# Row factors and diagonal blocks of a triangular matrix, taken chunk by chunk with the products that make it, in a hybrid decoder block on one Trainium2 core

## The chip, the cores and the metric

The kernel runs on one core of one Trainium2 chip. Its metric is device time in microseconds (us) of one execution. All times below are us unless they say ns.

## The reference, cut to what matters

One decoder layer over 512 tokens of width 1024: a combined input projection feeds three causal mixers (A: block-sparse attention, B: a chunked gated delta rule, C: sparse attention with an indexer that picks top keys), gates weigh their outputs, then come an output projection, a layer norm, and a squared-ReLU MLP with a second layer norm. The part at issue is mixer B, 4 heads of 128 columns. Per chunk it needs the inverse of a unit lower triangular matrix:

```python
q = to_chunks(q) * dk ** -0.5            # q, k are l2-normalised rows
diff = g[..., :, None] - g[..., None, :]
decay = jnp.where(causal, jnp.exp(jnp.where(causal, diff, 0.0)), 0.0)
kb = k * beta[..., None]
m = jnp.where(strict, -jnp.einsum('bhncd,bhnsd->bhncs', kb, k) * decay, 0.0)
tinv = lax.linalg.triangular_solve(eye - m, jnp.broadcast_to(eye, m.shape),
                                   left_side=True, lower=True, unit_diagonal=True)
u = jnp.einsum('bhncs,bhnse->bhnce', tinv, v * beta[..., None])
w = jnp.einsum('bhncs,bhnsd->bhncd', tinv, kb * jnp.exp(g)[..., None])
```

The kernel works with chunks of 128 tokens and unnormalised keys and queries, and puts the norms in as factors: a row factor beta / (k.k + eps) on the triangular matrix, and a factor on the query's result that is (q.q + eps) to the power -1/2, times 128 to the power -1/2.

## The kernel before, in words

**Matmuls and the stream.** Each large matmul is three fp32r matmuls (`mm3`, L91 to L93) on the high and low halves of both operands. `split` (L75) makes the halves of a weight: ACT casts (L76, tile `wh`), then DVE or POOL subtracts (L80, tile `wl`); `share` says how often POOL gets that. The projections are a stream of pieces: a piece loads one 128x1024 weight, runs 24 matmuls of 512 columns into a bank of `pj` (three buffers, as `wh` and `wl` have), and an eviction follows, for the gates an ACT operation on L173 (L176 for two of them). `weave(steps, n)` (L144) emits a list of steps with n pieces spread between them.

**Order.** Program order is only a priority. When the program is built, each engine's instructions are put into a fixed order by a scheduler that expects some duration of each: an instruction whose inputs are not yet expected lets later ones pass. On the chip each engine then works through its order, and waits at its head. So the top-k of the indexer (L413 and L414 on DVE), which comes later in the program, stands between the steps described here, and so do the halves of weights.

**The triangular stage**, for four chunks c of four heads each, 16 units u = 4c + h:

- `decays(c)` (L470) makes on DVE the masks R (L476), on PE the sums of log decays, on ACT their exponentials EA (L482, masked on POOL, L483) and EG (L488).
- `products(c)` (L492) has PE multiply keys with keys into the only `ov` bank (L499) and keys with queries into a `tr` bank (L501). DVE reads the diagonals of the first into `kk` (L503, one operation per head), multiplies by EA into LT (L505), and likewise into AT (L511). PE turns the queries (L508), ACT squares and sums them into `qq` (L510). DVE scales the queries by EG (L512). The steps are woven with GDEC = 2 pieces (L519).
- Behind the last chunk, DVE adds eps to `kk` and `qq` (L521, L522), takes the reciprocal and multiplies by beta (L523, L524: `br2`) and multiplies the four chunks of LT by it (L527). POOL raises `kk` to 1/2 (L529: `nk`) and `qq` to -1/2 (L530: `rq`); DVE scales `rq` by 128 to the -1/2 (L531); POOL multiplies the values by `nk` (L534).
- The 32x32 diagonal blocks of LT are copied into LD, doubled, by ACT and DVE, 32 partitions of 1024 elements each, two copies an engine (L543). DVE transposes LD into FB (L546) and runs 31 steps of forward substitution, two operations a step (L558, L560), into XB. Two transposes (L568, L570) give XY; ACT and DVE copy from it into XL (L572) and Y (L574).
- Only then does the program emit `weave([], GPRE)` (L576) with GPRE = 8 pieces. The levels of the block inverse follow, `q32` to `z64` (L584 to L617, the first product is L589), with two pieces between them, and the recurrence over the chunks (L626 to L686) with two more.

`rq` is used in the recurrence (L674), `nk` through the values (L648), `br2` in L652.

Of the kernel before, what the change touches and what calls it, by code (L numbers as in the profile page):

```python
# [10 lines left out]
F32 = mybir.dt.float32  # L11
F32R = mybir.dt.float32r
AF = mybir.ActivationFunctionType
OP = mybir.AluOpType
# [8 lines left out]
RMS_EPS = 1e-6  # L23
# [31 lines left out]
def hybrid_block(ctx, tc, xT, xn, wt, wva, wsm, wuk, wuv, wbr, wout, wup, wdn, relb, onehot, cmats,  # L55
                 convw, alog, dtb, gnorm, kvnorm, ikg, ikb, l1g, l1b, l2g, l2b, out):
    nc = tc.nc
    PE, DVE, ACT, POOL = nc.tensor, nc.vector, nc.scalar, nc.gpsimd
# [131 lines left out]
    gp = gctx.enter_context(tc.tile_pool(name="gp", bufs=1))  # L190
# [65 lines left out]
    v3 = lambda a: a.rearrange("p (h c) -> p h c", h=4)  # L256
# [81 lines left out]
    p = bank("pj")  # L338
# [6 lines left out]
    p = bank("tr")  # L345
# [7 lines left out]
    beta = const.tile([128, 16], F32, name="beta")  # L353
# [36 lines left out]
    for i in range(NT):  # L390
        DVE.tensor_scalar(kin[:, i, :64], sm[:, i, :64], kag[:, i, 0:1], krs[:, i:i + 1],
                          op0=OP.subtract, op1=OP.mult)
# [4 lines left out]
    p = bank("tr")  # L397
# [32 lines left out]
    for j in range(4):  # L430
        weave([lambda h=h, i=i: index_score(h, i) for h in (2 * j, 2 * j + 1) for i in range(1, NT)], 1)
        if j == 0:
            p = bank("tr")
# [23 lines left out]

    LT = gp.tile([128, 16, 128], F32, name="LT", tag="b8", bufs=4)
    AT = gp.tile([128, 16, 128], F32, name="AT", tag="b8", bufs=4)
    el = const.tile([128, 16], F32, name="el")  # L460

    scl = const.tile([128, 6, 16], F32, name="scl")
    kk, qq, nk, rq, br2 = (scl[:, i] for i in range(5))
    junk = gp.tile([128, 128], F32, name="junk")
    junk2 = gp.tile([128, 128], F32, name="junk2")
    hs = [slice(128 * h, 128 * h + 128) for h in range(4)]
# [25 lines left out]
    def products(c):  # L492
        cs = slice(128 * c, 128 * (c + 1))
        us = slice(4 * c, 4 * c + 4)
        EA, EG = dec[c]
        pQ = bank("tr")
        pK = bank("ov")
        for h in range(4):
            PE.matmul(pK[:, 128 * h:128 * h + 128], kT[:, h, cs], kT[:, h, cs], start=True, stop=True)  # L499
        for h in range(4):  # L500
            PE.matmul(pQ[:, 128 * h:128 * h + 128], kT[:, h, cs], qT[:, h, cs], start=True, stop=True)  # L501
        for h in range(4):
            DVE.scalar_tensor_tensor(junk, pK[:, hs[h]], 1.0, ident, op0=OP.mult, op1=OP.mult,  # L503
                                     accum_out=kk[:, 4 * c + h:4 * c + h + 1])
        DVE.tensor_tensor(LT[:, us], v3(pK), EA, OP.mult)  # L505
        p = bank("sc")
        for h in range(4):
            PE.transpose(p[:, hs[h]], qT[:, h, cs], ident)  # L508
        for h in range(4):
            ACT.activation(junk2, p[:, hs[h]], AF.Square, accum_out=qq[:, 4 * c + h:4 * c + h + 1])  # L510
        DVE.tensor_tensor(AT[:, us], v3(pQ), EA, OP.mult)  # L511
        DVE.tensor_tensor(qT[:, :, cs], qT[:, :, cs], EG, OP.mult)  # L512
# [5 lines left out]
    steps.insert(TV3, lambda: turn_value(3))  # L518
    weave(steps, GDEC)  # L519

    DVE.tensor_scalar(kk, kk, RMS_EPS, None, op0=OP.add)  # L521
    DVE.tensor_scalar(qq, qq, RMS_EPS, None, op0=OP.add)  # L522
    DVE.reciprocal(br2, kk)  # L523
    DVE.tensor_tensor(br2, br2, beta, OP.mult)  # L524
    for c in range(4):
        us = slice(4 * c, 4 * c + 4)
        DVE.tensor_tensor(LT[:, us], LT[:, us], bh(br2[:, us]), OP.mult)  # L527
    phalf, mhalf16 = pows[:, 0], pows[:, 1]
    POOL.tensor_tensor(nk, kk, phalf, OP.pow)  # L529
    POOL.tensor_tensor(rq, qq, mhalf16, OP.pow)  # L530
    DVE.tensor_scalar(rq, rq, 128.0 ** -0.5, None, op0=OP.mult)  # L531
    for c in range(4):
        us = slice(4 * c, 4 * c + 4)
        POOL.tensor_tensor(v3(vn[:, c]), v3(vn[:, c]), bh(nk[:, us]), OP.mult)  # L534
# [1 line left out]

    blk = [slice(32 * k, 32 * k + 32) for k in range(4)]
    LD = gp.tile([128, 32, 32], F32, name="LD", tag="LD")  # L540
    FB = gp.tile([128, 32, 32], F32, name="FB")
    for k, bs in enumerate(blk):
        (DVE.tensor_copy if k % 2 else ACT.copy)(  # L543
            LD[bs].rearrange("p c (h u) -> p c h u", h=2),
            LT[bs, :, bs].rearrange("p u c -> p c u")[:, :, None, :].to_broadcast([32, 32, 2, 16]))
    DVE.transpose(FB.rearrange("p c s -> p (c s)"), LD.rearrange("p c l -> p (c l)"))  # L546
    XB = gp.tile([128, 16, 32], F32, name="XB")
    TB = gp.tile([128, 512], F32, name="TB")
# [658 lines left out]
```

## Time and profile before

| what | value |
|---|---|
| median of 3 runs | 1024.02 us (1023.84 to 1025.14) |
| the profiled execution, its own time | 1024.51 us |
| its span, first to last instruction | 1022.7 us |
| mean granted PE clock | 0.968 |
| PE busy | 982.6 us, 96% of the span |
| DVE, ACT, POOL busy | 582.5, 416.6, 295.7 us |
| the chain that ended last, by engine | PE 74%, DVE 18%, ACT 3%, issue 2%, POOL 1%, DMA 1% |

The span is that of the profiled execution, and 1.8 us of its own time lie around it. A row of a timeline gives start, duration, engine, line, operation, output and inputs with their shapes, and in brackets how long the engine idled before it and what ended that. A row of the chain gives start, duration and what ran. Tile names are those of the program without buffer numbers; the views kk, qq, nk, rq and br2 show as their tile `scl`, the queries as `y_q_b` and the keys as `y_k_b`. Matmul ends are modelled and overlap the next start.

### The profile page before, as it was taken

To read this page: it belongs to the slowest core of one execution; us is meant where nothing else is said; L and a number is where in the kernel's file an instruction comes from. 1 tells how busy PE (TensorE), PEld (TensorE's weight loads), DVE (VectorE), ACT (ScalarE), POOL (GpSimd) and SP (SyncE) were. 2 spreads that over 40 slices of the span, in tenths; PEclk is the share of its full clock that TensorE was granted. 3 is DMA by queue.
4 is the path that set the end of the run, shared out by engine and by line. 5 is a ranking of instruction groups with operands and counts; after the bars stand their busy time and mean duration, and the time that the engine had idled before them with its cause. 6 is when DMAs were issued, how large, how long until landed. Compare 5 with 4: busy or idle time off the path is not lost.

```text
span 1022.7 us, 12939 instructions
## 1 busy us (share of the span) xinstructions
PE 982.6 (96%) x4868; PEld 807.7 (79%) x4868; DVE 582.5 (57%) x1145; ACT 416.6 (41%) x745; POOL 295.7 (29%) x194
## 2 busy tenths in 40 slices
PE   7999988979999999999999999999999999999997
PEld 4778876756788878878788888898888888888886
DVE  4969999793144657898975666842320222222236
ACT  4545435413124655776665353234332123333120
POOL 0202513521023223134443333224331013442111
PEclk9999998977599999999999999999999999999999
DMA  6385221133112321222334567223223323323312
GB/s 201 119 113 155 86 79 53 62 124 94 41 53 81 95 78 52 78 72 94 104 116 146 181 192 253 76 101 110 99 87 103 101 86 102 103 83 103 99 66 83
DMA packets 37931, 105.46 MB, mean 103 GB/s; under 512 B 5068, under 2 KB 9837, under 8 KB 37869
## 3 DMA queue, kind: packets, MB, share of 16 engines
q1 hardware_dynamic: 35804, 101.49, 30.1%
q10 hardware_dynamic: 2064, 3.15, 2.4%
q8 instruction: 38, 0.62, 0.2%
q14 instruction: 25, 0.20, 0.1%
HBM read 93.09 MB, written 11.53 MB: 102 GB/s over the span
## 4 chain that ended last, share of the span: by engine, by line
PE 74%; DVE 18%; ACT 3%; issue 2%; POOL 1%; DMA 1%; SPq 0%; DVEq 0%; ACTq 0%; POOLq 0%
PE pj L91 18%; PE pj L93 18%; PE pj L92 18%; DVE wl L80 2%; DVE isc L414 2%; DVE m L413 2%; PE sc L91 2%; PE sc L93 2%; PE sc L92 2%; PE tr L91 1%; PE tr L93 1%; PE tr L92 1%; PE tr L753 1%; PE sc L317 1%; PE sc L318 1%
## 5 line engine op out<-in xcount | busy, mean ns | idle before, releaser
L80 POOL TENSOR_TENSOR wl<-wraw,wh 128x1024 fp32r<-128x1024 f32 (+2 forms) x57 | 132.8, 2330 | 353.2 <-ACT wh L76 344.2
L76 ACT CAST wh<-wraw 128x1024 fp32r<-128x1024 f32 (+3 forms) x144 | 147.5, 1024 | 212.7 <-PE pj L92 101.5
L91 PE MATMUL pj<-xh,wh 128*128 128x512 f32 (+1 forms) x472 | 200.7, 426 | 3.4 <-ACT gate L173 2.0
L93 PE MATMUL pj<-xh,wl 128*128 128x512 f32 (+1 forms) x472 | 192.5, 408 | 8.0 <-DVE wl L80 6.3
L80 DVE TENSOR_TENSOR wl<-wraw,wh 128x1024 fp32r<-128x1024 f32 (+2 forms) x87 | 114.0, 1311 | 138.2 <-ACT wh L76 136.6
L92 PE MATMUL pj<-xl,wh 128*128 128x512 f32 (+1 forms) x472 | 190.8, 404 | 1.4 <-DVE xl L80 1.4
L93 PEld LDWEIGHTS pj<-xh,wl 128*128 128x128 f32 (+1 forms) x472 | 92.1, 195 | 31.1 <-DVE wl L80 8.1
L91 PEld LDWEIGHTS pj<-xh,wh 128*128 128x128 f32 (+1 forms) x472 | 91.7, 195 | 20.6 <-ACT gate L173 2.5
L92 PEld LDWEIGHTS pj<-xl,wh 128*128 128x128 f32 (+1 forms) x472 | 92.3, 196 | 16.3 <-DVE xl L80 3.3
L91 PE MATMUL pj<-x1h,wh 128*128 128x512 f32 (+1 forms) x280 | 104.0, 371 | 0.0
L92 PE MATMUL pj<-x1l,wh 128*128 128x512 f32 (+1 forms) x280 | 103.8, 371 | 0.0
L93 PE MATMUL pj<-x1h,wl 128*128 128x512 f32 (+1 forms) x280 | 103.8, 371 | 0.0
L1056 DVE TENSOR_TENSOR hl<-hraw,hh 128x512 fp32r<-128x512 f32 x32 | 22.2, 693 | 92.4 <-ACT hh L1055 92.4
L1053 POOL TENSOR_TENSOR hraw<-hraw 128x512 f32<-128x512 f32 x32 | 45.4, 1419 | 81.0 <-ACT hraw L1052 81.0
L93 PEld LDWEIGHTS pj<-x1h,wl 128*128 128x128 f32 x280 | 52.7, 188 | 9.1
L92 PEld LDWEIGHTS pj<-x1l,wh 128*128 128x128 f32 x280 | 52.8, 188 | 9.0
L91 PEld LDWEIGHTS pj<-x1h,wh 128*128 128x128 f32 x280 | 52.7, 188 | 9.0
L741 ACT ACTIVATE P<-P,ast 128x128 f32<-128x128 f32 (+1 forms) x64 | 36.0, 563 | 31.7 <-DVE ast L740 31.0
L1055 ACT CAST hh<-hraw 128x512 fp32r<-128x512 f32 x32 | 19.9, 621 | 67.6 <-POOL hraw L1053 67.6
L743 DVE TENSOR_SCALAR P<-P,ast 128x128 f32<-128x128 f32 (+1 forms) x64 | 34.5, 541 | 1.5
L736 POOL TENSOR_TENSOR bm<-strip,isc 128x256 f32<-128x256 f32 (+2 forms) x24 | 24.3, 1021 | 37.3 <-DVE ast L740 28.3
L759 DVE TENSOR_TENSOR ptl<-tr,pth 128x128 fp32r<-128x128 f32 (+1 forms) x64 | 30.5, 485 | 4.1 <-ACT pth L758 3.7
(376 smaller groups left out, 1990.5 us busy)
## 6 DMA issues: line engine op xcount, KB each, us to landing
wraw<-in_wt_dram SPq DMA_DIRECT2D x58, 512.0 KB, 3.3
wraw<-in_wup_dram SPq DMA_DIRECT2D x32, 512.0 KB, 3.3
wraw<-in_wdn_dram SPq DMA_DIRECT2D x32, 512.0 KB, 3.2
gdram<-gate SPq DMA_DIRECT2D x24, 256.0 KB, 2.0
wraw<-in_wbr_dram SPq DMA_DIRECT2D x12, 512.0 KB, 3.4
g<-gdram SPq DMA_DIRECT2D x24, 256.0 KB, 3.1
wraw<-in_wout_dram SPq DMA_DIRECT2D x8, 512.0 KB, 3.7
rrep<-rrow ACTq DMA_DIRECT2D x1, 3072.0 KB, 33.8
```

The lines of the kernel that those rows point to most:

```text
L76: ACT.copy(h, raw)
L80: eng.tensor_tensor(l, raw, h.bitcast(F32), OP.subtract)
L91: PE.matmul(out_ap, lh, rh, start=first, stop=False)
L92: PE.matmul(out_ap, lh, rl, start=False, stop=False)
L93: PE.matmul(out_ap, ll, rh, start=False, stop=last)
L413: DVE.max(m8, sc)
L736: POOL.tensor_tensor(bm[:, :n], bias, self.masks[i], OP.add)
L741: ACT.activation(P, P, AF.Exp, bias=mi[:, 0:1], scale=-1.0, accum_out=mi[:, 2:3])
L743: DVE.tensor_scalar(P, P, mi[:, 3:4], None, op0=OP.mult)
L759: DVE.tensor_tensor(dest(self.ptl), pv, dest(self.pth).bitcast(F32), OP.subtract)
L1053: POOL.tensor_tensor(a, a, a, OP.mult)
L1056: DVE.tensor_tensor(tl, a, th.bitcast(F32), OP.subtract)
```

## The change

The row factors br2 are made inside `products(c)` for the chunk's four columns, and the product of the keys is multiplied by its row factor and by EA in one operation per head. The chunk's part of the diagonal blocks is copied into LD there, by ACT (blocks 0 and 2) and by POOL (blocks 1 and 3; before: DVE), 32 partitions of 256 elements each. The four products behind the last chunk go, as do the common eps, reciprocal and beta operations. The factor 128 is multiplied into `qq` together with eps, ahead of the power -1/2, and L531 goes.

```diff
     LT = gp.tile([128, 16, 128], F32, name="LT", tag="b8", bufs=4)
     AT = gp.tile([128, 16, 128], F32, name="AT", tag="b8", bufs=4)
+    blk = [slice(32 * k, 32 * k + 32) for k in range(4)]
+    LD = gp.tile([128, 32, 32], F32, name="LD", tag="LD")
...
-        DVE.tensor_tensor(LT[:, us], v3(pK), EA, OP.mult)
+
+        DVE.tensor_scalar(kk[:, us], kk[:, us], RMS_EPS, None, op0=OP.add)
+        DVE.reciprocal(br2[:, us], kk[:, us])
+        DVE.tensor_tensor(br2[:, us], br2[:, us], beta[:, us], OP.mult)
+        for h in range(4):
+            u = 4 * c + h
+            DVE.scalar_tensor_tensor(LT[:, u], pK[:, hs[h]], br2[:, u:u + 1], EA[:, h], op0=OP.mult, op1=OP.mult)
+        for k, bs in enumerate(blk):
+            (POOL.tensor_copy if k % 2 else ACT.copy)(
+                LD[bs].rearrange("p c (h u) -> p c h u", h=2)[:, :, :, us],
+                LT[bs, us, bs].rearrange("p u c -> p c u")[:, :, None, :].to_broadcast([32, 32, 2, 4]))
...
-    DVE.tensor_scalar(kk, kk, RMS_EPS, None, op0=OP.add)
-    DVE.tensor_scalar(qq, qq, RMS_EPS, None, op0=OP.add)
-    DVE.reciprocal(br2, kk)
-    DVE.tensor_tensor(br2, br2, beta, OP.mult)
-    for c in range(4):
-        us = slice(4 * c, 4 * c + 4)
-        DVE.tensor_tensor(LT[:, us], LT[:, us], bh(br2[:, us]), OP.mult)
+    DVE.tensor_scalar(qq, qq, RMS_EPS, 128.0, op0=OP.add, op1=OP.mult)
     phalf, mhalf16 = pows[:, 0], pows[:, 1]
     POOL.tensor_tensor(nk, kk, phalf, OP.pow)
     POOL.tensor_tensor(rq, qq, mhalf16, OP.pow)
-    DVE.tensor_scalar(rq, rq, 128.0 ** -0.5, None, op0=OP.mult)
...
-    blk = [slice(32 * k, 32 * k + 32) for k in range(4)]
-    LD = gp.tile([128, 32, 32], F32, name="LD", tag="LD")
     FB = gp.tile([128, 32, 32], F32, name="FB")
-    for k, bs in enumerate(blk):
-        (DVE.tensor_copy if k % 2 else ACT.copy)(
-            LD[bs].rearrange("p c (h u) -> p c h u", h=2),
-            LT[bs, :, bs].rearrange("p u c -> p c u")[:, :, None, :].to_broadcast([32, 32, 2, 16]))
```

## Rows read from the trace of the kernel before

**Rows 1.** Timeline of PE, 177 to 238 us
```profile
177.81 1.16 PE L499 MATMUL ov<-y_k_b 128*128 128x128 f32 x8 [1.19 <-DVE LT L505]
...
198.20 0.50 PE L93 MATMUL pj<-xh,wl 128*128 128x512 f32 x1 [0.42 <-POOL wl L80]
...
205.04 0.50 PE L91 MATMUL pj<-xh,wh 128*128 128x512 f32 x1 [1.56 <-ACT gate L173]
...
206.99 0.79 PE L93 MATMUL pj<-xh,wl 128*128 128x512 f32 x1 [1.21 <-POOL wl L80]
...
208.86 0.63 PE L91 MATMUL pj<-xh,wh 128*128 128x512 f32 x1
...
218.74 0.80 PE L93 MATMUL pj<-xh,wl 128*128 128x512 f32 x1 [4.59 <-DVE wl L80]
...
236.84 0.39 PE L93 MATMUL pj<-xh,wl 128*128 128x512 f32 x1
237.16 0.43 PE L589 MATMUL sc<-XL,LT 32*32 32x32 f32 x8
```

**Rows 2.** Chain of waits, pieces between 184 and 218 us
```profile
184.12 3.89 POOL scl L529
...
193.59 5.70 DVE LT L527 x4
...
217.47 1.23 DVE wl L80
```

**Rows 3.** Timeline of ACT, 199 to 238 us
```profile
199.33 4.10 ACT L543 COPY LD<-LT 32x1024 f32<-32x1024 f32 x2 [10.11 <-DVE LT L527]
203.45 1.04 ACT L76 CAST wh<-wraw 128x1024 fp32r<-128x1024 f32 x1
...
213.56 1.05 ACT L76 CAST wh<-wraw 128x1024 fp32r<-128x1024 f32 x1 [5.70 <-PE pj L92]
...
232.95 2.21 ACT L572 COPY XL<-XY 32x512 f32<-32x512 f32 x2 [17.85 <-DVE XY L568]
...
236.46 1.05 ACT L76 CAST wh<-wraw 128x1024 fp32r<-128x1024 f32 x1
```

**Rows 4.** Timeline of DVE, 183 to 210 us
```profile
183.27 0.69 DVE L505 TENSOR_TENSOR LT<-ov,EA 128x512 f32<-128x512 f32 x1
183.87 0.17 DVE L521 TENSOR_SCALAR scl<-scl 128x16 f32<-128x16 f32 x1
...
190.92 1.01 DVE L531 TENSOR_SCALAR scl<-scl 128x16 f32<-128x16 f32 x1 [5.51 <-POOL scl L530]
...
203.57 1.23 DVE L546 STREAM_TRANSPOSE FB<-LD 128x1024 f32<-128x1024 f32 x1
...
207.46 2.39 DVE L558 TENSOR_TENSOR TB<-FB,XB 128x30 f32<-128x30 f32 x1
209.88 0.19 DVE L560 TENSOR_TENSOR XB<-XB,TB 128x30 f32<-128x30 f32 x1
```

**Rows 5.** Timeline of POOL, 190 to 210 us
```profile
190.86 4.49 POOL L534 TENSOR_TENSOR vn<-vn,scl 128x512 f32<-128x512 f32 x4
195.31 2.84 POOL L80 TENSOR_TENSOR wl<-wraw,wh 128x1024 fp32r<-128x1024 f32 x1
...
207.43 2.37 POOL L80 TENSOR_TENSOR wl<-wraw,wh 128x1024 fp32r<-128x1024 f32 x1 [0.50 <-ACT wh L76]
```

**Rows 6.** Groups: L503 and L727 (ns min/median/max), top-k from 184 us
```profile
L503 DVE SCALAR_TENSOR_TENSOR junk<-ov,cm x16: 267/280/1829, 156.4 to 183.1; 128x128 f32<-128x128 f32 x16
...
L413 DVE MAX8 m<-isc 128x8 f32<-128x512 f32 x3 | 2.1, 685 | 0.0
L414 DVE MATCH_REPLACE8 isc<-m,isc 128x512 f32<-128x512 f32 x3 | 2.0, 677 | 0.0
...
L727 POOL COPY strip<-far x16: 390/404/866, 317.6 to 521.6; 128x256 f32<-128x256 f32 x16
```

**Rows 7.** PE, PEld, DVE, ACT, POOL busy, PE clock, DMA share, GB/s, 245 to 281 us
```profile
245.00:281.00 36.00, 36.00 (x205) 25.02 (x204) 5.88 (x14) 5.81 (x12) 2.37 (x1) 0.50 0.14 49
```

## The prediction

> **What bounds the kernel now.** I read the page first: TensorE (PE) is the busiest engine by far, so the end moves only where PE idles or runs at its lower clock. I then read PE's timeline around the triangular stage for its idle gaps, the chain of waits for what stood behind them, and the timelines of ACT, DVE and POOL for what those had queued.
>
> PE works through eight stream pieces (24 matmuls each) between the products of chunk 3 and the first level product at 237.16, which starts right behind the last matmul of the eighth piece [rows 1]. So PE does not wait for the triangular chain there. It loses time earlier: 1.56 at 205.04 behind a gate eviction on ACT, 1.21 at 206.99 behind a `wl` on POOL, 4.59 at 218.74 behind a `wl` on DVE. After the second and third gaps the matmuls of 512 columns take 0.63 (the one at 208.86) against 0.39 at full clock (236.84) [rows 1]; 7 and 11 of them do. As each overlaps the next, I count 0.2 for one. A piece at full clock is 5.5: from 218.74 to 236.84 lie 69 matmuls, 11 of them slow, so (18.1 - 2.2) / 69 = 0.23 each, times 24.
>
> The chain of waits says why. From 184 to 217 it does not run through PE: two powers on POOL from 184.12 (3.89 the first), the four LT products (5.70), the substitution, and then the DVE `wl` that ends PE's longest gap [rows 2]. On ACT, the two LD copies wait 10.11 for LT and take 4.10, and the weight cast at 203.45 stands behind them; that makes the first two gaps [rows 3]. On DVE, L531 holds the queue for 5.51 until the second power is there, although only the query factor needs it, and the row factors of LT come after it [rows 4].
>
> **The change, part by part.**
>
> *Query factor inside the power.* L531 goes, 1.01 long, and with it the 5.51 that DVE waits [rows 4]; the 128 joins an existing operation, at no cost. The powers stay on POOL. What is late next is not DVE but the POOL queue.
>
> *Row factors with the products.* The four LT products (5.70) go [rows 2]. In their place each chunk has three operations on four columns (0.17 each by L521 [rows 4], 0.5 in sum) and four 128x128 products with a column scalar, priced by L503, the same form and shape, with a median of 280 ns [rows 6]: 1.1 in place of L505's 0.69 [rows 4]. That is 0.9 more per chunk, 2.7 before the keys' product of chunk 3, which already waits 1.19 for LT of chunk 2 to give its bank back [rows 1].
>
> *LD copies by chunk.* ACT's two copies, 4.10 for both at 32x1024 [rows 3], become eight of a quarter, 0.5 each; only chunk 3's pair, 1.0, remains behind the last LT. DVE's two go to POOL as eight. No row shows a POOL copy of 32 partitions with this stride; the nearest is the 128x256 copy, 0.39 to 0.87, median 0.40 [rows 6]. Bounds: 0 (hidden) and 0.87 each; I take 0.4, the median of the same element count. A POOL copy can also hold DVE up: the substitution product at 207.46 took 2.39 (the next, 0.19) while POOL's `wl` at 207.43 took 2.37 [rows 4, 5]. So the four copies of chunks 0 and 1 add 0 to 1.6 to DVE before chunk 3's keys.
>
> On this the Trainium skill ("SBUF — State Buffer", Who interferes with whom) speaks against the change: a DVE instruction with two SBUF inputs, or a copy in a two-port mode, and a GpSimd instruction that reads SBUF exclude each other for a whole instruction. The trace agrees, with 2.39 beside 2.37 [rows 4, 5]. By it all eight copies would stop DVE, about 3.2 us instead of my 1.6, if each fell on such an instruction, and the sum below would be up to 1.6 higher.
>
> *Where the chain then stands.* LT of chunk 3 ended at 183.96 [rows 4]; four times 0.9 and some contention put it at 188 to 190. With ACT's pair FB could start at 191. But the first power is ready before LT of chunk 3, so POOL probably takes it, perhaps both, ahead of its two copies: 6.7 for both (184.12 to the values at 190.86 [rows 2, 5]) from about 187, and 0.8 of copies, give 195; with the four value products (4.49 [rows 5]) in front as well, 199. FB started at 203.57 [rows 4]: 4.5 to 12 earlier, and I take 8. XL, copied from 232.95 to 235.16 [rows 3], is then there by 223 to 231, for a PE that wants it near 230: covered.
>
> *What PE gets.* (a) The gaps at 205.04 and 206.99 came from ACT standing in LD; they go, with 7 slow matmuls: 1.56 + 1.21 + 1.4 = 4.2 less. Bounds 0 and 4.2; the wait that made them is removed, so 4.2. (b) The `wl` at 217.47 sits in DVE's order among the substitution steps. If it keeps its place it comes 8 earlier and PE's 4.59 + 2.2 go; but a chain expected earlier puts more steps ahead of it. Bounds 0 and 6.8; I leave 1.5 standing and take 5.3 less. (c) The wait for chunk 3's keys grows by 0 (other matmuls put in front) to 4.3 (2.7 + 1.6); I take 1.5, nearer the low end, since PE has stream pieces to go on with. (d) POOL's `wl` at 195.31 stands behind the powers and the value products [rows 5], and PE already waits 0.42 for it [rows 1]; POOL begins them 2.7 later and has 0.8 of copies more, PE is 1.5 later itself: 0 to 3.5 less PE's own shift, I take 1.0.
>
> The sum: 4.2 + 5.3 - 1.5 - 1.0 = 7.0 less. From 237 on PE is nearly always busy, so this reaches the end. The profiled execution took 1024.51, 0.5 above the median of 1024.02: 1017.5.
>
> **The rivals.**
>
> *One cast stuck behind XL: no change.* ACT's XL copy now waits 17.85 for the substitution, and the cast at 236.46 stands behind it; the cast at 213.56 was the last ahead of it [rows 3]. Each engine's order is fixed when the program is built. If the chain is expected earlier by more than the distance between that cast and the XL copy, the cast of the eighth piece falls behind XL. Then XY at 225, XL 2.2, cast 1.05, `wl` 2.37 give weights near 230.6; PE wants them at 230 less one piece of 5.5, so it idles about 6 and has 2.2 of slow matmuls: 8 of loss against 7 of gain, 1025; with FB 12 earlier, 1021. Middle 1023. For it: it is the mechanism that LD shows now. Against: the order may move less than one cast.
>
> *Two casts behind XL: slower.* The same place, but the order shifts by over one piece (5.5), so that the seventh piece's weights wait too: PE idles about 11.4 and has 2.2 of slow matmuls, 13.6 against 7 of gain: 1031, or 1027 with FB 12 earlier. It decides from the point where two casts follow XL on ACT. Against it: LT, L531 and LD together must look over 5.5 us shorter to whoever orders the queues, and the products' stage gets longer.
>
> *DVE late in the products' stage.* The three small operations and the products depend on one another, and top-k operations of 0.68 can be let in between: six of them stand after 184 now [rows 6], so 4.1 can move ahead. With 2.7 and 1.6 that is 8.4 before chunk 3's keys; with 2.2 of slow matmuls and 1.0 from (d) it makes 11.6, against 11.0 from (a) and (b) in full: 1025.1. Against it: PE has stream pieces to put in front.
>
> *The clock of the level products.* From 245 to 281 the granted clock is 0.50, the level of 1.2 GHz, with PE busy for all 36.00 [rows 7], so some 18 could come back. Nothing in the change alters that mix; a shift of the order could move its beginning by some us.
>
> **How the numbers follow.** Forecast 0.48; one cast stuck 0.20; two casts 0.17; DVE late 0.10; the clock 0.05 (by 3 to 18 faster). About 0.2% is what a measurement of this kernel can tell from no change, 2 us. Faster: 0.48 + 0.05 + a third of the stuck cast, 0.60. Same: the rest of that rival and half of DVE late, 0.20. Slower: two casts and what is left, 0.20. The forecast's own range is 1012 (the waits of 1.19 and 0.42 gone too, 12.6 less) to 1021; the whole range, 1011 to 1027, takes in one stuck cast, late DVE and the lower edge of two.
>
> **What would show each step.** DVE without a wait for the powers and FB before 196: the chain is right; FB at 199 or later: POOL's queue holds its copies. The gate eviction no longer behind LD, and no gap near 205: (a). A `wl` gap under 2 in the substitution: (b). A keys' product waiting over 4 for LT: DVE late. ACT's cast straight after XL with PE idle before it: a stuck cast. The forecast is wrong if PE's gaps between 180 and the first level product still add up to 7 or more.

## The result, and the profile after

Four executions of the changed kernel took 1006.16, 1006.94, 1024.09 and 1024.38 (median 1015.51), beside 1023.34 to 1025.14 for the kernel before (median 1023.93). The comparison gives 0.9834 of the time before, interval 0.9809 to 0.9858; it rests on the two near 1006.5, and a number in the middle, such as the median, is one that no execution took. The mean granted clock of PE parts the two pairs: 0.987 and 0.966. The kernel before showed one group only: 69 executions beside the runs below, 1021.46 to 1027.78, clock 0.963 to 0.971.

The profiled execution of the changed kernel is one of the upper pair: own time 1024.38, span 1022.4, clock 0.967, PE busy 982.6 again. So it shows what the change did to the chain, and where that was lost. Its line numbers are shifted by the edit: LT is on L513, the LD copies on L515, the powers on L535 and L536, the values on L539, FB on L545, the substitution on L557, XL on L571, Y on L573, the first level product on L588 and the first product of the recurrence on L629.

PE's timeline, 146 to 277, to be set against [rows 1] (L501 is the product of keys with keys, chunks 0, 2 and 3 in turn):

```profile
146.62 1.05 PE L501 MATMUL ov<-y_k_b 128*128 128x128 f32 x8
...
175.12 1.16 PE L501 MATMUL ov<-y_k_b 128*128 128x128 f32 x8 [1.97 <-DVE LT L513]
...
177.08 0.78 PE L487 MATMUL sc<-R,cr 128*128 128x512 f32 x1 [0.57 <-ACT EA L484]
...
186.51 1.05 PE L501 MATMUL ov<-y_k_b 128*128 128x128 f32 x8
...
214.43 0.61 PE L93 MATMUL pj<-xh,wl 128*128 128x512 f32 x1 [4.18 <-DVE wl L80]
...
232.12 0.43 PE L588 MATMUL sc<-XL,LT 32*32 32x32 f32 x8
234.47 0.50 PE L91 MATMUL pj<-xh,wh 128*128 128x512 f32 x1 [1.92 <-ACT gate L173]
234.81 0.40 PE L92 MATMUL pj<-xl,wh 128*128 128x512 f32 x1
235.24 0.79 PE L93 MATMUL pj<-xh,wl 128*128 128x512 f32 x1
...
276.69 1.05 PE L629 MATMUL tr<-cm,y_k_b 128*128 128x128 f32 x4
```

The gaps near 198, 205 and 207 are gone. The wait of a keys' product for its bank is not: it has moved from chunk 3 (1.19 [rows 1]) to chunk 2 (1.97), with 0.57 for EA behind it. Nor is the gap behind DVE's `wl`: 4.18 where it was 4.59. The first level product starts at 232.12 against 237.16 [rows 1], 5.04 earlier. Two matmuls after a gap of 1.92 the 512-column matmuls take 0.79 in place of 0.40, and the recurrence begins at 276.69. In the kernel before, the keys' product of chunk 0, the two waits behind the first level product and the beginning of the recurrence stand so:

```profile
148.20 1.05 PE L499 MATMUL ov<-y_k_b 128*128 128x128 f32 x8
...
238.05 0.50 PE L91 MATMUL pj<-xh,wh 128*128 128x512 f32 x1 [0.46 <-ACT gate L173]
...
241.20 0.59 PE L589 MATMUL sc<-XL,LT 32*32 32x32 f32 x13 [0.39 <-ACT Q L591]
...
277.43 1.05 PE L630 MATMUL tr<-cm,y_k_b 128*128 128x128 f32 x4
```

Not all of the 5.04 is the chain's: 1.58 are there at the keys' product of chunk 0 (146.62 against 148.20), the first product of the stage that the change edits. From 70 to 75 the mean granted clock reads 0.66 in the kernel before and 1.00 in the changed one; in lev3_plain below, the changed kernel but for one constant, it reads 0.66 there as well, so that fall comes and goes without the change. For the chain 3.46 are left. Of the 5.04 there is 0.74 left 45 us later, and 0.3 at the end of the span. I call the stretch from the first level product to the first recurrence product the level stage; it took 40.27 before and 44.57 after. The windows of the changed kernel show why (columns as in [rows 7]: PE, PEld, DVE, ACT, POOL busy, PE clock, DMA share, GB/s):

```profile
232.00:234.00 2.00, 0.56 (x9) 0.32 (x8) 0.04 (x1) 1.96 (x4) 0.00 (x0) 1.00 0.00 0
234.00:236.00 2.00, 1.50 (x4) 0.62 (x5) 1.18 (x1) 2.00 (x4) 0.56 (x1) 0.79 0.35 130
236.00:238.00 2.00, 2.00 (x13) 1.61 (x12) 0.00 (x0) 1.71 (x4) 2.00 (x2) 0.50 0.89 169
...
275.00:280.00 5.00, 5.00 (x22) 4.20 (x21) 1.11 (x2) 1.64 (x2) 2.33 (x1) 0.55 0.14 52
```

and those of the kernel before, on either side of the stretch in [rows 7]:

```profile
240.00:245.00 5.00, 4.61 (x64) 3.02 (x62) 1.12 (x4) 1.81 (x6) 3.71 (x2) 0.92 0.97 273
...
280.00:285.00 5.00, 5.00 (x31) 4.60 (x31) 1.98 (x3) 0.59 (x1) 0.78 (x1) 0.82 0.41 143
```

A window's clock gives the moment at which it fell or rose: 0.92 over 5 us is 0.8 at 0.50 and the rest at 1.00. So the 1.2 GHz level lasted from 244.2 to 281.8 before (37.6) and from 235.2 to 279.5 after (44.3). At that level the work takes about twice as long, so half of the difference, 3.3, is time lost; with the gap of 1.92 in place of two of 0.46 and 0.39 that is 4.4, about the 4.30 by which the stage got longer. In this execution the lower clock, and for a smaller part the gap, took back nearly all of what had been gained ahead of the stage. In the two near 1006.5 the mean clock says that the long fall did not come: 0.02 of some 1020 us is 20 us of clock, or 40 us at 0.50, about this stretch.

The rest of the chain, on ACT, DVE and POOL of the changed kernel, against [rows 3], [rows 4] and [rows 5]:

```profile
194.43 1.31 ACT L515 COPY LD<-LT 32x256 f32<-32x256 f32 x2 [3.53 <-DVE LT L513]
195.77 0.60 ACT L173 ACTIVATE gate<-pj 128x512 f32<-128x512 f32 x1
...
229.38 2.23 ACT L571 COPY XL<-XY 32x512 f32<-32x512 f32 x2 [18.19 <-DVE XY L567]
231.62 1.24 ACT L573 COPY Y<-XY 32x512 f32<-32x512 f32 x2
232.88 1.04 ACT L76 CAST wh<-wraw 128x1024 fp32r<-128x1024 f32 x1
233.83 0.59 ACT L173 ACTIVATE gate<-pj 128x512 f32<-128x512 f32 x1
```

```profile
193.27 1.13 DVE L513 SCALAR_TENSOR_TENSOR LT<-ov,scl,EA 128x128 f32<-128x128 f32 x4
201.24 1.25 DVE L545 STREAM_TRANSPOSE FB<-LD 128x1024 f32<-128x1024 f32 x1 [6.84 <-POOL LD L515]
...
210.82 2.42 DVE L557 TENSOR_TENSOR TB<-FB,XB 128x110 f32<-128x110 f32 x1
213.16 1.21 DVE L80 TENSOR_TENSOR wl<-wraw,wh 128x1024 fp32r<-128x1024 f32 x1
```

```profile
192.65 3.06 POOL L535 TENSOR_TENSOR scl<-scl,pows 128x16 f32<-128x16 f32 x1 [0.19 <-DVE scl L508]
195.79 4.04 POOL L539 TENSOR_TENSOR vn<-vn,scl 128x512 f32<-128x512 f32 x4
199.90 1.31 POOL L515 COPY LD<-LT 32x256 f32<-32x256 f32 x2
...
210.77 2.34 POOL L80 TENSOR_TENSOR wl<-wraw,wh 128x1024 fp32r<-128x1024 f32 x1 [3.00 <-ACT wh L76]
```

LT of chunk 3 is ready at 194.40 and ACT's pair of copies at 195.74, yet FB waits 6.84 for POOL's pair, which stand behind a power (3.06) and the four value products (4.04). FB comes at 201.24 against 203.57 [rows 4], 2.33 earlier.

### The profile page after: what moved, and what is told of

It is laid out like the page before. It is cut to its first block, busy times and chain, and to the rows that moved or that the text cites. A ratio compares the mean times of both kernels' runs of the same rounds, so it can differ in the third digit from the quotient of the medians.

```text
span 1022.4 us, 12968 instructions
## 1 busy us (share of the span) xinstructions
PE 982.6 (96%) x4868; PEld 807.8 (79%) x4868; DVE 573.7 (56%) x1159; ACT 418.1 (41%) x751; POOL 300.3 (29%) x202
## 4 chain that ended last, share of the span: by engine, by line
PE 72%; DVE 16%; ACT 4%; DMA 3%; issue 2%; POOL 2%; SPq 0%; DVEq 0%; ACTq 0%; POOLq 0%
PE pj L91 18%; PE pj L93 17%; PE pj L92 17%; DMA wraw<-in_wt_dram 3%; DVE wl L80 2%; DVE isc L414 2%; DVE m L413 2%; PE sc L92 2%; PE sc L93 2%; PE sc L91 2%; PE tr L92 1%; PE tr L93 1%; PE tr L91 1%; PE tr L752 1%; PE ov L92 1%
## 5 line engine op out<-in xcount | busy, mean ns | idle before, releaser
L80 DVE TENSOR_TENSOR wl<-wraw,wh 128x1024 fp32r<-128x1024 f32 (+2 forms) x87 | 111.5, 1282 | 138.5 <-ACT wh L76 137.0
L1055 DVE TENSOR_TENSOR hl<-hraw,hh 128x512 fp32r<-128x512 f32 x32 | 22.2, 692 | 92.4 <-ACT hh L1054 92.4
```

Of the source, the lines that this page charges most:

```text
L80: eng.tensor_tensor(l, raw, h.bitcast(F32), OP.subtract)
L1055: DVE.tensor_tensor(tl, a, th.bitcast(F32), OP.subtract)
```

## The experiments

Three theories. **Clock**: PE's granted clock in the level stage sets the time; the mix of work there decides whether it holds (theory 1 in the expectations that number them, C or C2 in those with letters). **Chain**: the shortened triangular chain itself is what pays (theory 2, or D). **Gap**: PE's idle time at the beginning of the level stage makes the clock fall (theory 3, or C1). "Pieces" are stream pieces of 24 matmuls. "Held" counts executions with a mean clock of 0.98 or more. All kernels compute the whole layer; each was timed beside the kernel before. The ratios don't treat the two groups alike (y_dve's mixes them, y_dve_again's rests on the executions that held), so the times beside them are what to read.

| kernel | held | times where it held | other times | ratio to before |
|---|---|---|---|---|
| changed, both looks | 3 of 9 | 1006.2 to 1006.9 | 1022.0 to 1025.4 | 0.9834 [0.9809, 0.9858], first look |
| q_only | 0 of 5 | | 1018.0 to 1020.9 | 0.9955 [0.9941, 0.9970] |
| rows_only | 0 of 9 | | 1019.5 to 1022.8 | 0.9966 [0.9955, 0.9977] |
| copies_dve | 0 of 11 | | 1019.7 to 1023.6 | 0.9981 [0.9971, 0.9991] |
| y_dve | 3 of 6 | 1003.4 to 1004.7 | 1018.9 to 1019.6 | 0.9887 [0.9833, 0.9941] |
| y_dve_again | 4 of 7 | 1002.0 to 1003.8 | 1018.7 to 1019.5 | 0.9790 [0.9771, 0.9810] |
| y_before | 4 of 12 | 1006.4 to 1009.0 | 1018.4 to 1022.0 | 0.9904 [0.9868, 0.9939] |
| lev3_before | 4 of 4 | 1007.4 to 1010.0 | | 0.9851 [0.9833, 0.9870] |
| lev3_plain | 5 of 5 | 1007.0 to 1011.8 | | 0.9853 [0.9833, 0.9874] |
| lev4_before | 4 of 4 | 1009.2 to 1014.0 | | 0.9869 [0.9848, 0.9890] |
| lev4_after | 4 of 6 | 1007.6 to 1012.8 | 1017.8, 1019.3 | 0.9880 [0.9846, 0.9915] |
| lev3_after | 4 of 4 | 1013.2 to 1015.1 | | 0.9896 [0.9879, 0.9913] |
| lev1_after | 0 of 5 | | 1009.2 to 1014.9 | 0.9881 [0.9861, 0.9902] |
| best_a | 5 of 5 | 1003.8 to 1006.9 | | 0.9811 [0.9794, 0.9828] |
| best_b | 4 of 4 | 1001.7 to 1006.9 | | 0.9800 [0.9779, 0.9821] |
| best_c | 4 of 4 | 1005.1 to 1009.6 | | 0.9828 [0.9807, 0.9849] |
| best_d | 4 of 4 | 1012.4 to 1014.8 | | 0.9900 [0.9886, 0.9914] |
| best_e | 5 of 5 | 1005.9 to 1009.4 | | 0.9837 [0.9823, 0.9852] |

**The changed kernel once more, unaltered** (after_again).

> The changed kernel once more, unaltered, for a profile of an execution near 1006. Theory C (the clock of the level products): its executions lie in two groups, near 1006 and 1024, with mean granted clocks near 0.987 and 0.967; a profile of the lower group shows the level stage, which the profile at 1024.4 had at half clock from 235 to 280, at full clock for most of that stretch, and ends about 18 earlier there; before 232 both profiles agree within 1. Theory D (the chain): the lower group gained ahead of the first level product, which then starts 10 or more before the 232.1 of the upper group.

One of five executions held (1006.62; a sixth, of 3370.47, is left out). The profiled one, again of the upper group, had FB at 200.48, a `wl` gap of only 1.20, and the first level product at 229.98, 7.2 earlier than before; the recurrence began at 276.18, 1.25 earlier. A better chain than in the first profile (1.37 of the 7.2 are there at the keys' product of chunk 0), and the same time: what PE no longer waits for `wl`, it waits at the beginning of the level stage, for XL and for the gate eviction behind it.

```profile
229.98 0.63 PE L588 MATMUL sc<-XL,LT 32*32 32x32 f32 x8 [2.09 <-ACT XL L571]
233.87 0.79 PE L91 MATMUL pj<-xh,wh 128*128 128x512 f32 x1 [3.26 <-ACT gate L173]
```

No profile of an execution near 1006 came of it, so it does not decide between the two theories.

**The parts alone.** q_only is the kernel before with the query factor inside the power:

```diff
-    DVE.tensor_scalar(qq, qq, RMS_EPS, None, op0=OP.add)
+    DVE.tensor_scalar(qq, qq, RMS_EPS, 128.0, op0=OP.add, op1=OP.mult)
...
-    DVE.tensor_scalar(rq, rq, 128.0 ** -0.5, None, op0=OP.mult)
```

> Only the factor 128 inside the power; LT, LD as in the kernel before. Theory D: DVE no longer waits 5.5 for the powers, FB starts about 6 earlier (near 197.5), PE's gaps near 205 to 219 shrink, 3 to 7 less: 1017 to 1021, in one group. Theory C: PE's gain ahead of the level products is 0 to 5, and executions fall in two groups 15 to 20 apart only if the level stage is met at full clock; 1019 to 1024 in one group, or some near 1003 to 1006 with a granted clock near 0.987.

rows_only is the kernel before with the row factors in `products(c)`, the copies left behind the last chunk as they were:

```diff
-        DVE.tensor_tensor(LT[:, us], v3(pK), EA, OP.mult)
+        DVE.tensor_scalar(kk[:, us], kk[:, us], RMS_EPS, None, op0=OP.add)
+        DVE.reciprocal(br2[:, us], kk[:, us])
+        DVE.tensor_tensor(br2[:, us], br2[:, us], beta[:, us], OP.mult)
+        for h in range(4):
+            u = 4 * c + h
+            DVE.scalar_tensor_tensor(LT[:, u], pK[:, hs[h]], br2[:, u:u + 1], EA[:, h], op0=OP.mult, op1=OP.mult)
```

> Only the row factors inside the products; LD copied behind them as before, the query factor still by DVE behind the power. Theory D: the four LT products (5.7) leave the chain, while DVE's wait for the powers no longer stands ahead of LD; FB near 196 to 200, 3 to 7 less, one group. Theory C: the same shift moves the first level product by 0 to 5 and the time by that much, unless the level stage is met at full clock: then a group 15 to 20 lower with a granted clock near 0.987.

copies_dve is the changed kernel with the odd diagonal blocks copied by DVE in place of POOL:

```diff
-            (POOL.tensor_copy if k % 2 else ACT.copy)(
+            (DVE.tensor_copy if k % 2 else ACT.copy)(
```

> The changed kernel with blocks 1 and 3 of LD copied by DVE in each chunk and not by POOL. The power and the value products on POOL then no longer stand ahead of chunk 3's copies: FB starts right behind LT and ACT's pair, near 195 to 196 and not at 201.2. Theory D: the first level product or the time follows by 2 to 5. Theory C: PE still has its eight pieces to do, so the first level product stays within 2 of 232.1, and the time is again one of two groups near 1006 and 1024, the shares of which may differ.

| kernel (profiled execution) | FB starts | level stage starts | recurrence starts | median time |
|---|---|---|---|---|
| before | 203.57 | 237.16 | 277.43 | 1023.87 (beside these runs) |
| changed | 201.24 | 232.12 | 276.69 | 1022.0 to 1025.4, where the clock fell |
| q_only | 193.40 | 227.34 | 273.55 | 1019.35 |
| rows_only | 196.66 | 228.12 | 274.44 | 1020.25 |
| copies_dve | 197.87 | 229.95 | 276.69 | 1022.45 |

In all three FB comes earlier than in the whole change. It goes with POOL's queue: q_only and rows_only ask nothing new of POOL, and taking the copies off POOL brings FB 3.4 earlier. The end follows the start of the recurrence and not that of the level stage: 9.8 earlier there is 3.9 earlier here and 4.5 at the end (q_only). As long as the clock falls, the chain pays less than half of what it brings. Part of that is idle time and not clock: in the three profiles PE waits 1.27, 4.80 and 2.42 for XL ahead of the first level product, and 3.46, 2.32 and 3.39 behind it for a gate eviction or a cast, where the kernel before waits 0.46. In none of these 25 executions did the clock hold, although all three chains are shorter than the changed kernel's: the chain theory doesn't explain 1006. The times of q_only and rows_only lie where both theories had put them and don't part the two. For copies_dve both had FB at 195 to 196, and it came at 197.87; the first level product came 2.2 earlier than in the changed kernel, on the edge between the two forecasts, and the group near 1006 that the clock theory expected did not show in eleven executions.

**Taking the gap away, and filling the stage.** In the changed kernel the gate eviction that ends the gap stands on ACT behind XL, two copies into Y and a cast. y_dve gives all four Y copies to DVE:

```diff
-    for k, f in enumerate((DVE.tensor_copy, ACT.copy, ACT.copy, DVE.tensor_copy)):
+    for k, f in enumerate((DVE.tensor_copy, DVE.tensor_copy, DVE.tensor_copy, DVE.tensor_copy)):
```

> The changed kernel with all four copies of Y by DVE, so that ACT reaches the cast and the gate eviction behind XL 1.24 earlier and PE's gap after the first level product (1.92 in the profile at 1024.4) shrinks or goes. Theory C1 (the gap at the start of the level stage makes the clock fall there): most executions now near 1006, granted clock near 0.987. Theory C2 (the mix of small products and three stream matmuls a step is what cannot hold the clock): the fall stays, executions mainly near 1020 to 1024, the share near 1006 no larger than 3 of 10.

Half of the executions held, where theory C1 (gap) had asked for most and C2 (mix) had allowed three in ten. The profiled one (own time 1003.44) held; its PE timeline and windows:

```profile
232.65 0.43 PE L588 MATMUL sc<-XL,LT 32*32 32x32 f32 x8
...
258.34 0.60 PE L629 MATMUL tr<-cm,y_k_b 128*128 128x128 f32 x4
```

```profile
234.00:236.00 2.00, 1.75 (x14) 1.03 (x14) 0.00 (x0) 1.98 (x5) 2.00 (x1) 1.00 0.87 215
...
240.00:245.00 5.00, 5.00 (x63) 3.37 (x64) 0.86 (x3) 0.89 (x3) 0.00 (x0) 1.00 0.36 133
245.00:250.00 5.00, 5.00 (x73) 3.61 (x70) 2.21 (x4) 2.44 (x5) 0.00 (x0) 1.00 0.23 70
250.00:255.00 5.00, 5.00 (x39) 3.48 (x37) 0.99 (x3) 0.83 (x3) 0.00 (x0) 1.00 0.24 91
```

The level stage starts half a microsecond later than in the changed kernel's profile, with the `wl` gap still at 4.56, and takes 25.69 in place of 44.57: 18.88 of the 20.94 between the two own times lie there. That is the clock theory's place and size; y_dve_again below shows the same with one kernel in both groups.

lev3_after, lev4_after and lev4_before put three or four pieces between the level products, at the cost of the last stretch of the kernel (lev4_before is lev4_after's edit on the kernel before; lev3_after has `GLEV = 3`, `GMID = 5` and a last 2 in `GSEG`):

```diff
-GSEG = (1, 0, 1, 0, 2, 1, 2, 3)
+GSEG = (1, 0, 1, 0, 2, 1, 2, 1)
-GMID = 4
-GLEV = 2
+GMID = 6
+GLEV = 4
```

> The changed kernel with three stream pieces among the level products in place of two (4.5 stream matmuls a step in place of 3), one gate piece fewer at the end of mixer A and C's heads. The work is the same. Theory C1: as the changed kernel, two groups, since the gap at the start stays. Theory C2: PE's clock holds or comes back in the level stage; more than half of the executions below 1012, and the profile's level stage has granted clock near 1.0 in most slices.

> The same with four pieces among the level products (6 stream matmuls a step), two gate pieces fewer later. Theory C1: two groups as the changed kernel. Theory C2: all executions below 1012, none near 1023; granted clock near 0.985 or above.

> The kernel before with four pieces among the level products. Theory C2: the level stage runs at full clock here too, so that the time falls from 1024 by 12 to 18 without any of the change, to 1006 to 1012; the difference to the changed kernel with four pieces is then the chain's own gain, 0 to 5. Theory C1: no gain, 1020 to 1026, since before the level stage of the kernel before there is no gap to remove. Theory D (the chain's shortening is what pays in the fast executions): 1020 to 1026 here, while the changed kernel with four pieces stays as it was.

With four pieces the kernel before holds its clock in all four executions and is 11 to 16 below the median beside it, 1024.89, with none of the change in it. The piece taken from the last stretch is missed there (best_d below prices it), which is why lev3_after is above lev3_plain, and above the 1012 that most of its executions were forecast to stay under. lev4_after missed: two of six did not hold, and in its profiled one (1017.83) the clock fell at the beginning of the stage, at 234.6, and came back within it, but only at 258.5. So four pieces make a long fall rarer and don't rule it out.

**Apart: the change, the Y copies and the pieces.** y_before is the kernel before with y_dve's edit. best_a is y_dve with `GLEV = 3` alone, so that the piece comes from the recurrence; best_b adds the edit of copies_dve; best_c is q_only with the two.

> The kernel before, with all four copies into Y made by DVE (two of them were ACT's). Theory 1 (PE's granted clock in the stage of the level products sets the time, and whether it falls hangs on the kernel's own mix of work there): the unaltered stage has two pieces of 512-column matmuls, so most executions stay near 1020 to 1025 with a mean clock of 0.97; an execution that keeps the clock would be some 18 shorter, near 1004 to 1007. Theory 2 (the shortened triangular chain itself is what pays): no execution below 1018. Theory 3 (PE's gap at the beginning of the stage makes the clock fall): the kernel before has no gap there, so 1020 to 1025 in all, and nothing changes.

> The changed kernel, with the copies into Y by DVE and three pieces in place of two between the level products (one fewer in the recurrence). Theory 1 (clock of the level stage): nearly all executions keep 1.00 through the stage, 1001 to 1008. Theory 2 (the chain pays, the clock is chance): two groups as in the changed kernel, 1003 to 1006 and 1019 to 1024. Theory 3 (the gap at the beginning): no gap over 1, so full clock, 1001 to 1008 as well.

> As the kernel with three pieces and Y by DVE, and in addition the odd diagonal blocks copied by DVE in place of POOL. Theory 1: full clock as without it, 1001 to 1008, and FB some 3 earlier moves the time by less than 2, since PE has pieces in front. Theory 2: the earlier FB shows as 3 less than the kernel with POOL's copies.

> The kernel before with the query factor alone taken inside the power, Y by DVE and three pieces between the level products. Theory 1: full clock, 1003 to 1011, near the changed kernel with the same two additions; what is left between the two is the chain's own worth, 0 to 5. Theory 2: at least 5 above the changed kernel with the same additions.

In y_before eight of twelve stayed above and four held. Theory 1 allowed for such an execution, without saying that there would be so many; theories 2 and 3 forecast none. So it takes no change of the chain to bring some executions over: moving 1.2 of copies from ACT to DVE does (four of twelve, where none of the 69 of the kernel before held). The three with three pieces held in all 13 executions, and there the chain's worth can be read: best_c 1006.37, best_a 1005.46, best_b 1003.60. That is 1 to 3 for the row factors and copies, with intervals that overlap.

**One constant.** lev3_before and lev3_plain are the kernel before and the changed kernel with `GLEV = 3`; lev1_after is the changed kernel with `GLEV = 1`. y_dve_again is y_dve.

```diff
-GLEV = 2
+GLEV = 3
```

> The kernel before with one constant altered: three pieces in place of two between the level products, one fewer in the recurrence; the same number in all. Theory 1 (the pieces in the stage decide the clock): 1005 to 1012 in nearly all executions, without any of the change. Theory 2 (the shortened chain pays): 1020 to 1026, no difference.

> The changed kernel with that constant alone altered. PE's gap at the beginning of the stage (1.9 to 3.3 in the changed kernel) is still there. Theory 1 (pieces): 1003 to 1010 in nearly all executions. Theory 3 (the gap makes the clock fall and keeps it down): two groups as in the changed kernel, near 1006 and near 1022.

> The changed kernel with one piece in place of two between the level products, one more in the recurrence. Theory 1 (pieces): the clock falls in all executions, none below 1015. Theory 2 or chance: two groups as in the changed kernel, some three in ten near 1006.

> The changed kernel with the four copies into Y by DVE once more (3 of 6 executions were near 1004, 3 near 1019). Theory 3 (the gap decides): with the gap at 0.3, most executions near 1004. Theory 1: as without it, two pieces are at the edge and both groups come again, some 3 to 5 in 10 near 1004.

lev3_before: 1009.09; lev3_plain: 1007.97; the intervals are nearly the same. One digit in the kernel before brings 15, and with it in both kernels the change is worth 1.1, which these runs can't tell from nothing. In lev3_before's profile 3.36 of the gain stand ahead of the level stage (first level product at 233.80), some of it the fall from 70 to 75, which this execution did not have; the stage and the piece that moved into it bring the rest. lev3_plain keeps its gap, and the clock does fall after it, but comes back within the stage, 3.4 later (235.4 to 238.8). Its PE timeline and windows:

```profile
235.26 0.67 PE L91 MATMUL pj<-xh,wh 128*128 128x512 f32 x1 [2.06 <-ACT gate L173]
```

```profile
234.00:236.00 2.00, 0.73 (x2) 0.37 (x2) 1.23 (x1) 2.00 (x3) 0.00 (x0) 0.86 0.00 0
236.00:238.00 2.00, 2.00 (x5) 1.16 (x4) 0.00 (x0) 2.00 (x4) 1.78 (x1) 0.50 0.88 256
238.00:240.00 2.00, 2.00 (x21) 1.38 (x21) 0.30 (x1) 0.59 (x3) 2.00 (x2) 0.79 1.10 316
240.00:245.00 5.00, 5.00 (x67) 3.45 (x69) 1.16 (x4) 0.53 (x2) 0.93 (x1) 1.00 0.74 246
```

y_dve_again's profiled execution (1019.13) is one that did not hold. Here the clock falls behind a wait for XL, comes back by 237, and falls a second time at 240.5, with PE busy since 232.97:

```profile
230.33 0.63 PE L588 MATMUL sc<-XL,LT 32*32 32x32 f32 x8 [2.13 <-ACT XL L571]
...
232.97 0.79 PE L91 MATMUL pj<-xh,wh 128*128 128x512 f32 x1 [2.01 <-ACT gate L173]
...
273.24 1.05 PE L629 MATMUL tr<-cm,y_k_b 128*128 128x128 f32 x4
```

```profile
232.00:234.00 2.00, 1.03 (x3) 0.59 (x3) 1.81 (x3) 2.00 (x4) 0.07 (x1) 0.50 0.11 42
...
236.00:238.00 2.00, 2.00 (x35) 1.28 (x34) 0.28 (x2) 0.22 (x2) 2.00 (x2) 0.73 0.93 307
238.00:240.00 2.00, 2.00 (x26) 1.37 (x22) 0.84 (x4) 0.48 (x2) 0.61 (x1) 1.00 0.71 261
240.00:245.00 5.00, 5.00 (x46) 3.34 (x44) 0.87 (x3) 0.32 (x2) 0.00 (x0) 0.55 0.41 150
```

This is the same kernel as y_dve, in the other group: its level stage takes 42.91 (230.33 to 273.24) where y_dve's took 25.69, and these 17.22 cover the 15.69 between the two own times. From 500 to 980 every window of 20 us reads 1.00 in both, so it is this stage that is slower and not the whole execution.

So a gap can bring a fall, but it isn't what keeps the clock down, and here the long fall comes without one: as the only cause of the 20 us the gap theory falls. That rests on this one trace; in the other profiles with a long fall a wait of PE of 0.2 to 5 us stands ahead of it. Nor did moving the copies take the gap away every time: in y_dve PE waits 0.25 there in all, here 2.13 and 2.01. Seven of the 13 executions of y_dve's kernel held, three of nine of the changed kernel; with so few, whether the smaller gap helps stays open.

lev1_after is a miss for theory 1: no execution held, as it said, but all are below 1015 and the median is 1011.29. Its windows:

```profile
238.00:240.00 2.00, 2.00 (x28) 1.24 (x21) 1.21 (x5) 0.36 (x2) 0.91 (x1) 0.78 0.88 269
240.00:245.00 5.00, 5.00 (x56) 3.67 (x55) 0.76 (x3) 0.89 (x3) 0.00 (x0) 0.50 0.39 147
...
255.00:260.00 5.00, 5.00 (x23) 3.82 (x22) 2.36 (x4) 1.96 (x3) 0.00 (x0) 0.54 0.14 52
```

With one piece the fall lasts from 239.1 to 259.6, 20.5 in place of 44.3, since the stage ends sooner: the piece that left it runs at full clock in the recurrence. So the rule "more pieces, better" is wrong. What costs is how long PE works at the lower level, and two pieces are the worst of one, two and three: enough to make the stage long, and in most executions too few for the clock to come back in it.

**A ninth piece ahead of the stage.** best_b makes PE wait 2.14 for XL and 2.21 for the gate eviction at the beginning of the stage. best_d takes one piece from the last stretch to cover that, best_e from the recurrence:

```diff
-GPRE = 8
+GPRE = 9
```

> The changed kernel with both sets of odd copies by DVE, three pieces between the level products and a ninth piece ahead of them (taken from the last stretch of the kernel). Theory 1 with a covered chain: PE's waits at the beginning of the stage go, the clock stays at 1.00 for nearly all of it, and up to 4 of the time without the ninth piece (1003.6) go: 999 to 1004, unless the last stretch misses the piece it gave up. If the piece is missed there, 1004 to 1010.

> The same with the ninth piece taken from the recurrence, which has none left. Theory 1 with a covered chain: 999 to 1004 if the recurrence fills PE without it; if it doesn't, PE waits there and the time is 1004 to 1012.

best_d missed, at 1013.71; best_e, at 1007.95, lies in the second of its two ranges, the one for a recurrence that doesn't fill PE (its last wait there is 3.16, in best_b 1.20). Neither comes to the 999 to 1004 of a covered chain, with the clock held (0.986 to 0.989). The level stage moves back to 238.39 and 240.35, XL is covered, and PE waits 4.78 and 5.11 for a gate eviction instead, which stands behind XL on ACT here too. The piece taken from the last stretch costs 5.8 more than the one from the recurrence. best_b stays the best of all that ran: 1003.60, 0.9800 of the kernel before.

## Why the prediction was right and wrong

The forecast was 1017.5 and "faster"; it is, by 17, in the three of nine executions that held, while the other six, 1022.0 to 1025.4, lie within the range of the kernel before. 1017.5 lies between the two groups and describes neither; that it is close to the median of the first four, 1015.51, is chance.

**The step that failed** is the sentence behind the sum: "From 237 on PE is nearly always busy, so this reaches the end." Of 5.04 brought to the first level product, 0.3 reached the end in the profiled execution, because PE was as busy as forecast, at half the clock, and for longer. The stretch ahead of it is not what failed: by the prediction's own sign PE's gaps between 180 and the first level product would have had to come to 7, and they came to 4.18, from 7.78. And the sum has no term for the clock of the level stage, which by the mean clock is what the 17 in the executions that held are. The rival that held the answer, the clock of the level products, had the right stretch and the right size ("some 18 could come back": 18.88 came back in the level stage of y_dve) and a chance of 0.05, for the reason that "nothing in the change alters that mix". The pieces and products of the stage are indeed the same; the clock went otherwise in a third of the executions all the same. The row read 0.50 over 36 us in the one execution that had a trace [rows 7]; that another execution of the same program could read 1.00 there was not considered.

On that the Trainium skill ("TensorE: Matmul & The Clock Gate", What's actually happening) says that the lower level is the default and that activity releases the throttle. As far as the busy time of a profile tells activity, this case's trace does not bear that out as it stands: PE has no idle time from 245 to 281 and stays at 0.50 [rows 7], and y_dve's profiled execution, with the same products and the same two pieces, is at 1.00 through the stage. The Trainium skill's price for such a stretch (same page, HAM oscillation — how this bites in real kernels) is half of the throttled time. By that an estimate for the 44.3 is 22.2, and the own times of the changed kernel and y_dve differ by 20.94, so the trace roughly agrees.

By terms:

- **(a), 4.2 less: right.** No gap is left at 205 and 207; ACT's gate eviction at 195.77 comes straight behind a short pair of copies.
- **(b), 5.3 less: mis-sized.** In the profile it is about 1 (4.59 to 4.18, and some three slow matmuls fewer behind it). FB moved by 2.33 and not by 8, the `wl` that PE waits for by 4.31 (213.16 against 217.47 [rows 2]), and PE, which gets there 3.90 earlier itself (210.25 against 214.15), wants it that much sooner. In both kernels a substitution step that runs beside a POOL `wl` stands right ahead of it in DVE's queue: 2.42 beside 2.34 here (210.82 and 210.77), 2.31 beside 2.34 before (214.84 and 214.68), where such a step alone takes 0.2 to 0.4. The Trainium skill ("SBUF — State Buffer", Who interferes with whom) states that exclusion, and these rows agree. In the second look DVE's `wl`, at 210.42, came ahead of POOL's at 211.01, and 1.20 of the gap was left. There (b) came to 3.4, and the wait for XL took it back.
- **(c), 1.5 more: too low.** I looked for it at chunk 3, whose keys' product at 186.51 waits for nothing. It came at chunk 2: 1.97 for LT in place of the 1.19, 0.57 for EA, and a clock of 0.52 from 177 to 180 behind the two, some 1.6: about 3.0 in sum.
- **(d), 1.0 more: nothing of it shows**; no gap near 198.
- **The chain.** LT of chunk 3 was forecast for 188 to 190 and came at 194.40, since its keys' product itself stands 8.70 later (186.51 against 177.81 [rows 1]), with stream pieces in front of it. FB was forecast at 195.5 and came at 201.24, and the sign given for that ("FB at 199 or later: POOL's queue holds its copies") is what the rows show: 3.06 and 4.04 in front of them. A POOL copy of a quarter took 0.65 (1.31 for two), not the 0.4 of a row of another shape [rows 6]; ACT's took 0.65, not 0.5.

The sum to the first level product, 7.0 forecast and 3.46 found beside the 1.58 from ahead of the stage, is sound in kind and half in size. That XL is covered held in the first profile by 0.5 (its copies end at 231.61) and failed in the second look, where PE waits 2.09 for it. The two rivals with stuck casts did not come: XL on ACT has the cast behind it at 232.88, but PE's loss there is 1.92 for a gate eviction, not 6 for weights. Their mechanism, work that PE needs behind XL on ACT, is the one that shows, and in the second look the two waits come to 5.35. DVE late did come in part: LT of chunk 1 made PE's 1.97 at chunk 2; LT of chunk 3, at 194.40, cost PE nothing itself.

What is shown: the place and size of the two groups (level stage, 17.22 within one kernel), that the change isn't needed for the gain (lev3_before), that with three pieces all 35 executions of either kernel held, that POOL's copies delay FB. What stays open: why two pieces leave it to the execution, why the kernel before is always on the wrong side of that and the changed one in two executions of three, and whether the shorter gap shifts the share.

## What to carry to other kernels

Where a stage reads 0.50 with PE busy, price it first: up to half of its length is the prize (here 17.22 of 42.91), and moving one piece of large matmuls into or out of the stage is a one-constant experiment that here was worth 15 us against 1 for a careful rebuild of the chain in front of it. A gain ahead of such a stage must not be carried to the end at par, and before an edit is believed, run it several times and look at the mean clock of every execution, since a small shift of the order can change the share of executions that keep it. A copy moved to a queue that has slow work in it arrives behind that work, however short it is itself.

## What the runs showed of the hardware

- The same program on the same data ended in two groups some 13 to 18 us apart, near 0.987 and 0.97 in mean clock, with nothing between (the changed kernel, y_dve, y_before).
- A stage of 32x32 and 64x64 products with two pieces of 512-column matmuls stayed at 0.50 for 34 to 51 us in eight profiles, with PE busy but for waits in the first 9 us at most, and in a ninth (y_dve) at 1.00 throughout. With three pieces the mean clock was 0.98 or more in all 35 executions (eight kernels), and their profiles have 3.4 to 10.2 us at 0.50 there; with four, one profile (lev4_after) has 23.9 and one (lev4_before) none.
- The clock fell from 1.00 to 0.50 with no idle time of PE ahead of it for over 7 us (at 240.5 in y_dve_again, PE busy since 232.97 by the profile).
- A DVE substitution step took 2.3 to 2.5 beside a POOL subtraction of 2.3 to 2.9, and 0.2 to 0.4 without one; whether DVE's own subtraction came before or behind such a step differed between executions of the changed kernel, and with it PE's gap (1.20 or 4.18).
- A power of 128x16 elements on POOL took 2.9 to 4.1, three to four times as long as a product of 128x512 (1.0 for each of the values).
